# A transformer block on one core: the attention branch's output product as a Strassen product, with operands prepared in the projections and kept in DRAM

## The chip, the cores and the metric

The kernel runs on one core of one Trainium2 chip. The metric is device microseconds (us) from one launch to its end. Before the change three runs gave 1318.06, 1318.31 and 1318.65 us; the median is 1318.31 us.

## What is computed

One residual block of a streaming encoder: 1024 positions, width 1024, float32. Every sub-layer is normalised before and after.

```python
proj = h @ w_in                       # q, k, v, f, g_b, g_c, hc, gate_conv, gate_attn
ya = g_b * conv3(g_c * hc)            # [1024, 512]
yb = forgetting_attention(q, k, v, logf)              # [1024, 512]
ya_d = ya @ w_branch[0]               # branch a, [1024, 512] x [512, 1024]
yb_d = yb @ w_branch[1]               # branch b, [1024, 512] x [512, 1024]
merged = sigmoid(gate_conv) * ya_d + sigmoid(gate_attn) * yb_d
x = x + rmsnorm(merged @ w_out)       # then a SwiGLU feed-forward, same pattern
```

## The kernel before

Activations lie transposed: width on the 128 partitions, positions along the free axis in two halves of 512 (`n1`, `n2`). Each float32 operand is split into a rounded part `hi` and a rest `lo` (`split`, lines 131 to 134: a copy on ScalarE, ACT, and a subtraction on VectorE, DVE). A product is then three matmuls, hi·hi, hi·lo, lo·hi (`mm3`, lines 136 to 142). The large products (projections, w_out, feed-forward) are Strassen products in Winograd's form: a 2 x 2 block product from seven block products, with sums of weight blocks S1 to S4 and of activation blocks T1 to T4. The names A11, B21, T2 and so on are those blocks.

**Projections** (the loop at lines 999 to 1086). Seventeen jobs and a last one of another form. Job 0 to 3 makes a pair of q and k tiles, 4, 5, 7 and 8 the convolution's input (`z`), 6 and 9 its gate (`gb`), and 10 to 17 the two output gates. Each job is a Strassen product of seven times 12 matmuls, 128 x 512 each (`strassen`, lines 639 to 665). TensorE (PE) writes into PSUM banks b1, b2 and b3, and DVE adds these into c12, c22 and c21; bank b2 is rewritten by product S3 after DVE has taken S2's result out. While a job runs, DVE also prepares the next job's weight sums, and `wo_load` (lines 963 to 988) prepares a piece of w_out: four loads of 128 x 128, four sums for T1 to T4, one split, two stores to `wo_dram`. The finished output gates are stored to `sg_dram` (lines 1073 to 1082).

**Attention** (lines 1090 to 1360) works through steps t. Two tables, `cuts` and `at`, say in which step a side work is done: the splits of branch a's operands, the loads of the gates, and in steps 19 to 25 the loads and splits of branch b's four weight tiles (`load_wb`, `split_wb`).

**Branch b** (lines 1448 to 1471). For each half n and each of 8 width tiles d: load the gate `sg` from `sg_dram` (tiles from four buffers, line 1107), 12 matmuls into a fresh PSUM bank `pbb`, then on DVE `sg = sg * pbb` and `um += sg`. In the first half, `cut_wo` loads and splits the plain blocks B11 and B21 of w_out; in the second half the prepared T2 and T1 are loaded. After tile 1 of the second half come `first_ops(0)`, which splits the first blocks of `um`, and `sums(0)`, four sums over `um` on GpSimd (POOL).

**w_out** (lines 1517 on). `first(i)` is the product A11·B11 of position pair i into a bank `p1`, `second(i)` A12·B21 into a bank `q`, four pairs in all. Then come transposes and the other five products. B22 is loaded and split at lines 1622 to 1627.

Each engine executes its own instructions in order. A scheduler chooses that order from dependencies and priorities, except where `strict` (lines 64 to 81) names an engine: its instructions then keep the program's order. Tiles come from pools of fixed size; a tile waits until the last reader of the buffer's previous tile is done. All recorded operations have the line of one helper, so the profile shows nearly everything as L76 (L77 after the change), and groups are told apart by tile names.

Of the kernel before, what the change touches and what calls it, by code (L numbers as in the profile page):

```python
# [10 lines left out]
F32 = mybir.dt.float32  # L11
# [31 lines left out]
B11, B21, B22, T1, T2, T3, T4 = range(7)  # L43


@with_exitstack
def block_kernel(
# [58 lines left out]
    def f32(ap):  # L106
        return ap.bitcast(F32)
# [23 lines left out]
    def split(hi, lo, src):  # L131

        copy(hi, src)
        sub(lo, src, f32(hi))
# [25 lines left out]
    wo_dram = dpool.tile([4, 4, P, 2, NC], F32, name="wo_dram")  # L160
# [802 lines left out]
    def wo_load(n):  # L963
# [12 lines left out]
        def cut():  # L976
            for o, a, b in ((4, 0, 1), (5, 3, 4), (6, 3, 0), (7, 2, 5)):
                sub(r[:, o], r[:, a], r[:, b])
            split(h[:, 4:], l[:, 4:], r[:, 4:])

        def store():
            for hl, t in enumerate((h, l)):
                nc.scalar.dma_start(
                    wo_dram[:, k, :, hl, c * P : (c + 1) * P].rearrange("o p m -> p o m"),
                    f32(t[:, 4:]),
                )
# [3 lines left out]
    side = {}  # L990
# [8 lines left out]
    for ij, (kind, j, _, _) in enumerate(jobs):  # L999
        mid = None  # L1000
        if ij in side:
            cut, store = side.pop(ij)
            mid = do(pinned, cut, "vector", "scalar")
# [79 lines left out]
        if mid is not None:  # L1083
            pinned(store, "scalar")
        if ij < len(jobs) - 2:
            side[ij + 1] = wo_load(ij)
# [8 lines left out]
    yb = yb_pool.tile([P, 4, S], F32, name="yb")  # L1095
# [140 lines left out]
    wbr = {}  # L1236
    wbh, wbl = [], []
# [6 lines left out]

    def load_wb(k):
        wbr[k] = flat(wtile("sx", 1) if k == 3 else raw_t())
        nc.sync.dma_start(wbr[k], w_branch[0, 1][k * P : (k + 1) * P, :])

    def split_wb(k):
        wbh.append(flat(hi_t()))  # L1250
        wbl.append(z_tile("wbl", F32R) if k == 1 else flat(lo_t()))
        return halve(wbh[k], wbl[k], wbr[k])
# [13 lines left out]
    for k, t in enumerate((20, 22, 24, 25)):  # L1266
        cuts[t].append(do(split_wb, k))
# [10 lines left out]
    for k in range(4):  # L1278
        at[19].append(do(load_wb, k))
# [88 lines left out]
    def yb_split(n, ks):  # L1368
        ns = (n1, n2)[n]
        for k in ks:  # L1370
            split(yb2[n][0][:, k, :], yb2[n][1][:, k, :], yb[:, k, ns])

    for m in branch_a(KT - 1, 0, psm, "mm"):
        pass
    for n in range(2):
        nc.scalar.activation(sgs[KT - 1, n], sgs[KT - 1, n], AF.Sigmoid)
    m()
    yb2 = [halves_of(0)]
    for m in branch_a(KT - 2, 1, psm, "mm"):
        pass  # L1380
    yb_split(0, (0, 1))
    m()
    for m in branch_a(KT - 1, 1, psm, "mm"):
        pass
    divide(3, 0)
    yb_split(0, (2, 3))
    m()
    divide(3, 1)
    yb2.append(halves_of(1))
    yb_split(1, range(4))  # L1390
    strict[0] = ()
    yb_close()
    wx, wx_close = pool("wx", side="right")

    def x_tile(n, p=None):
        return (p or wx).tile([P, 2, 4, NC], F32R, tag=f"x{n}", name=f"x{n}", bufs=1)
# [6 lines left out]
    def load_wo(o, k):  # L1403
        nc.sync.dma_start(f32(wo[o][:, :, k, :]), wo_dram[o - T1, k])

    def cut_wo(w, ops):
        for h, (o, row, cols) in enumerate(ops):
            wr = w[:, (n1, n2)[h]]
            nc.sync.dma_start(wr, wout_d[row * P : (row + 1) * P, cols])
            split(*(wo[o][:, hl, row % 4, :] for hl in range(2)), wr)  # L1410

    for n, o in enumerate((B11, B21, T2, T1)):
        wo[o] = x_tile(n)
    loads = [(o, k) for o in (T2, T1) for k in range(4)]
# [19 lines left out]

    def minus(i, o, a, b, op=ALU.subtract):
        e = nc.vector if i else nc.gpsimd
        e.tensor_tensor(o, a, b, op=op)
# [9 lines left out]

    for n in range(2):
        ns = slice(n * NC, (n + 1) * NC)
        for d in range(KT):  # L1450
            ds_ = slice(d * P, (d + 1) * P)
            sg = sg_tile()
            nc.sync.dma_start(sg, sg_dram[d][1, :, ns])
            if n:
                load_wo(*loads.pop(0))
            elif d % 2 == 0:
                cut_wo(flat(raw_t()), ((B11, d // 2, n1), (B21, 4 + d // 2, n1)))
            if d == KT - 1:
                nc.scalar.activation(sg, sg, AF.Sigmoid)
            ps = psm.tile([P, NC], F32, tag="mm", name="pbb")  # L1460
            for k in range(4):
                mm3(
                    ps, (wbh[k][:, ds_], wbl[k][:, ds_]),
                    (yb2[n][0][:, k, :], yb2[n][1][:, k, :]),
                    k == 0, k == 3,
                )
            mul(sg, sg, ps)
            add(um[:, d, ns], um[:, d, ns], sg)
            if n and d == 1:
                first_ops(0, [s4h_t(), s4h_t()], [s4l_t(), s4l_t()])  # L1470
                sums(0, s4_t())
# [153 lines left out]
    for k in (0, 2):  # L1625
        w = ep.tile([P, D], F32, tag="t", name="wr", bufs=1)
        cut_wo(w, ((B22, 4 + k, n2), (B22, 5 + k, n2)))
# [177 lines left out]
    wx_close()  # L1805

# [250 lines left out]
```

## Time and profile before

| what | value |
| --- | --- |
| median of three runs | 1318.31 us |
| span of the profiled execution | 1316.7 us |
| that execution's time outside the span, if it ran at the median | 1.6 us |
| PE busy | 99% |
| DVE busy | 73% |
| ACT busy | 42% |
| POOL busy | 11% |
| mean rate of DMA | 160 GB/s |

The profile is of one execution. Its page gives busy shares by engine and the chain of work that ended last; the trace gives each instruction's start and duration. The listed duration of a matmul is longer than the distance to the next one, since they are pipelined; the distance is what counts. DVE's listed durations overlap in the same way by about 0.1 us.

### The profile page before, as it was taken

Reading aid. Unit: us, or ns where it says so; the run is one execution under the profiler, and the core shown is the slowest. Engines: PE = TensorE matmul, PEld = TensorE weight load, DVE = VectorE, ACT = ScalarE, POOL = GpSimd, SP = SyncE. Lnnn points to the kernel's source line nnn. Section 1 sums busy time; section 2 is a strip of 40 time slices with the busy share of each in tenths; the row PEclk is TensorE's granted clock in tenths of the full one; section 3 lists DMA queues with packets and bytes.
Section 4 is the critical chain, followed back from the end, with each engine's and each line's share of the span. In section 5 each row is a group of like instructions: output and inputs, shape, how many; then the busy total and the mean of one; then the engine's idle time right before and its main releaser. Section 6 shows DMA issues by size and latency. Waiting matters only on the chain.

```text
span 1316.7 us, 17979 instructions
## 1 busy us (share of the span) xinstructions
PE 1307.0 (99%) x6710; PEld 1090.6 (83%) x6710; DVE 964.2 (73%) x1514; ACT 556.4 (42%) x895; POOL 142.0 (11%) x271
## 2 busy tenths in 40 slices
PE   9999999999999999999999999999999999999997
PEld 9988888888888888888888888888888888888886
DVE  6974878765656876776798789987766776676685
ACT  6642322243355866514677522222222234444452
POOL 0001000011012212010012021221001110000000
PEclk9999999999999999999999999999999999999999
DMA  6344544555536545565266555553323337866441
GB/s 215 115 120 136 149 124 121 155 159 150 152 120 200 162 137 175 160 226 208 79 227 206 155 166 176 179 181 104 98 86 120 105 112 285 311 252 193 159 168 64
DMA packets 189351, 211.00 MB, mean 160 GB/s; under 512 B 11584, under 2 KB 137600, under 8 KB 189264
## 3 DMA queue, kind: packets, MB, share of 16 engines
q1 hardware_dynamic: 155872, 146.64, 35.8%
q0 software_dynamic: 16496, 54.83, 11.3%
q10 hardware_dynamic: 16896, 8.39, 2.1%
q8 instruction: 52, 0.85, 0.3%
q14 instruction: 35, 0.29, 0.1%
HBM read 151.30 MB, written 58.52 MB: 159 GB/s over the span
## 4 chain that ended last, share of the span: by engine, by line
PE 95%; DVE 2%; ACT 1%; DMA 1%; issue 0%; DVEq 0%; POOL 0%; ACTq 0%; SPq 0%; POOLq 0%
PE b L76 57%; PE pd L76 16%; PE pbb L76 3%; PE pba L76 3%; PE pv L76 3%; PE po L76 2%; PE tps L76 2%; PE p L76 2%; PE sp L76 2%; PE ma L76 1%; PE tp L76 1%; PE q L76 1%; DMA lo<-qk_dram 1%; PE mb L76 1%; PE spin L76 1%
## 5 line engine op out<-in xcount | busy, mean ns | idle before, releaser
L76 PE MATMUL b<-x,hi 128*128 128x512 f32 x1088 | 335.3, 389 | 0.0
L76 PEld LDWEIGHTS b<-x,hi 128*128 128x128 f32 x1088 | 204.2, 188 | 42.1
L76 PE MATMUL b<-x,lo 128*128 128x512 f32 x544 | 211.7, 389 | 0.0
L76 DVE TENSOR_TENSOR c<-c,b 128x512 f32<-128x512 f32 x193 | 131.8, 683 | 62.1 <-PE b L76 54.6
L76 DVE TENSOR_TENSOR lo<-raw,hi 128x1024 fp32r<-128x1024 f32 x92 | 110.9, 1205 | 76.7 <-PE b L76 66.8
L76 ACT ACTIVATE hi<-raw 128x1024 fp32r<-128x1024 f32 (+1 forms) x99 | 100.5, 1018 | 97.4 <-PE b L76 51.2
L76 PEld LDWEIGHTS b<-x,lo 128*128 128x128 f32 x544 | 102.2, 188 | 21.2
L76 ACT ACTIVATE hi<-sx 128x1024 fp32r<-128x1024 f32 (+1 forms) x43 | 44.9, 1043 | 152.5 <-PE b L76 144.8
L76 ACT ACTIVATE sgf<-c 128x512 f32<-128x512 f32 x31 | 19.6, 633 | 131.8 <-DVE c L76 112.6
L76 DVE TENSOR_TENSOR lo<-sx,hi 128x1024 fp32r<-128x1024 f32 (+1 forms) x43 | 51.5, 1199 | 30.7 <-PE b L76 27.3
L76 DVE TENSOR_TENSOR sx<-raw 128x512 f32<-128x512 f32 x78 | 53.6, 688 | 14.2 <-DMA raw<-in_w_gate_up_dram 6.9
L76 PE MATMUL pd<-hi,lo 128*128 128x512 f32 x160 | 62.3, 389 | 0.0
L76 PE MATMUL pd<-hi 128*128 128x512 f32 x160 | 61.9, 390 | 0.0
L76 PE MATMUL pd<-ghi 128*128 128x512 f32 x148 | 57.6, 390 | 0.0
L76 PE MATMUL pd<-glo,ghi 128*128 128x512 f32 x148 | 57.6, 389 | 0.0
L76 PE MATMUL pd<-ghi,glo 128*128 128x512 f32 x148 | 57.6, 389 | 0.0
L76 PE MATMUL b<-hT34h,lo 128*128 128x512 f32 x136 | 52.9, 389 | 0.0
L76 PE MATMUL b<-hT34h,hi 128*128 128x512 f32 x136 | 52.9, 389 | 0.0
L76 PE MATMUL b<-hT34l,hi 128*128 128x512 f32 x136 | 52.9, 389 | 0.0
L76 PE MATMUL b<-hT12h,hi 128*128 128x512 f32 x136 | 52.9, 389 | 0.0
L76 PE MATMUL b<-hT12l,hi 128*128 128x512 f32 x136 | 52.9, 389 | 0.0
L76 PE MATMUL b<-hT12h,lo 128*128 128x512 f32 x136 | 52.9, 389 | 0.0
(425 smaller groups left out, 3018.3 us busy)
## 6 DMA issues: line engine op xcount, KB each, us to landing
raw<-in_w_gate_up_dram SPq DMA_DIRECT2D x55, 512.0 KB, 3.9
raw<-in_w_in_dram SPq DMA_DIRECT2D x35, 512.0 KB, 4.3
a_dramS<-um POOLq DMA_DIRECT2D x44, 256.0 KB, 3.0
a_dramA<-um POOLq DMA_DIRECT2D x33, 256.0 KB, 2.7
sg<-sg_dram SPq DMA_DIRECT2D x32, 256.0 KB, 3.8
x<-wo_dram SPq DMA_DIRECT2D x16, 512.0 KB, 6.1
graw<-a_dramS SPq DMA_DIRECT2D x14, 512.0 KB, 4.2
sg_dram<-c POOLq DMA_DIRECT2D x24, 256.0 KB, 3.5
```

The lines of the kernel that those rows point to most:

```text
L76: ins = getattr(self.engine, name)(*args, **kw)
```

## The change

Branch b becomes a Strassen product. Its 2 x 2 blocks are: width outputs even and odd tiles, positions `n1` and `n2`, and the 512 inputs in two halves. The seven block products (four width tiles u, two input tiles, three matmuls each, so 24 matmuls) stand in the order A11·B11, S1·T1, S2·T2, S3·T3, S4·B22, A22·T4, A12·B21; TensorE keeps the program's order in them. They accumulate in eight PSUM banks, `pbanks` (tiles `pbp`) and `vbanks` (tiles `pbv`).

Weight blocks: `wb_load` prepares A11, A12, A22 and S1 to S4 in jobs 2 to 9 (four loads of 64 KB, four 128 x 128 sums, a split of 128 x 896, two stores to `wb_dram`); `load_wbr` loads them. `wo_load` splits and stores all seven blocks of w_out, 128 x 896 where it was 128 x 512, and `load_wo` loads B11, B21 and B22 as finished halves, so `cut_wo` is gone. Activation blocks T1 to T4 are formed in place in `yb` on DVE, T1 in attention steps 20 and 22. The T1 block of w_out is loaded into the space of `yb`, its T2 block into that of the temporaries.

```diff
-    wo_dram = dpool.tile([4, 4, P, 2, NC], F32, name="wo_dram")
+    wo_dram = dpool.tile([7, 4, P, 2, NC], F32, name="wo_dram")
+    wb_dram = dpool.tile([7, 2, P, 4, 2, P], F32, name="wb_dram")
...
-            split(h[:, 4:], l[:, 4:], r[:, 4:])
+            split(h[:, 1:], l[:, 1:], r[:, 1:])
...
+    def wb_load(n):
...
+        def cut():
+            add(r[:, 4], r[:, 0], r[:, 3])
+            sub(r[:, 6], r[:, 1], r[:, 0])
+            sub(r[:, 5], r[:, 4], r[:, 1])
+            sub(r[:, 7], r[:, 2], r[:, 5])
+            split(h[:, 1:], l[:, 1:], r[:, 1:])
...
         if ij < len(jobs) - 2:
-            side[ij + 1] = wo_load(ij)
+            side[ij + 1].append(wo_load(ij))
+        if 1 <= ij < 9:
+            side[ij + 1].append(wb_load(ij - 1))
...
+    def load_wbr(o):
+        h = hi_t()
+        l = kblk(z_tile("wbl", F32R)) if o == S1 else lo_t()
+        wb[o] = h, l
+        for hl, t in enumerate((h, l)):
+            nc.sync.dma_start(
+                f32(t).rearrange("p (u k) m -> p u k m", u=4), wb_dram[o, hl]
+            )
...
-    for k, t in enumerate((20, 22, 24, 25)):
-        cuts[t].append(do(split_wb, k))
+    cuts[20].append(cut_b11)
+    cuts[22].append(cut_t1)
...
-    for k in range(4):
-        at[19].append(do(load_wb, k))
+    at[20].append(form_t1)
+    for o, t in ((A11, 19), (S1, 20), (S2, 24), (S3, 25)):
+        at[t].append(do(load_wbr, o))
...
+    def prod_b(ps, o, u, b, first):
+        (wh, wl), (bh, bl) = wb[o], tb[b]
+        kw = {} if first else dict(skip_group_check=True)
+        for k in range(2):
+            m = 2 * u + k
+            mm3(
+                ps, (wh[:, m, :], wl[:, m, :]), (bh[:, k, :], bl[:, k, :]),
+                first and k == 0, k == 1, **kw,
+            )
+
+    def merge(d, ns, t, c, sg):
+        mul(t, c, sg)
+        add(um[:, d, ns], um[:, d, ns], t)
...
+    for u in range(4):
+        prod_b(pbanks[u], S2, u, T2, False)
+        copy(u_s[u], pbanks[u])
+    load_wbr(A12)
+    for u in range(4):
+        sg = gate(2 * u + 1, n1)
+        prod_b(pbanks[u], S3, u, T3, False)
+        add(v_s[u], v_s[u], pbanks[u])
+        merge(2 * u + 1, n1, v_s[u], v_s[u], sg)
+    for u in range(4):
+        sg = gate(2 * u, n1)
+        prod_b(vbanks[u], S4, u, B22, False)
+        add(u_s[u], u_s[u], vbanks[u])
+        copy(vbanks[u], p_s[u])
+        merge(2 * u, n1, u_s[u], u_s[u], sg)
+        load_wo(B21, u)
+    first_ops(0, [s4h_t(), s4h_t()], [s4l_t(), s4l_t()])
+    sums(0, s4_t())
+    for u in range(4):
+        sg = gate(2 * u + 1, n2)
+        prod_b(pbanks[u], A22, u, T4, False)
+        merge(2 * u + 1, n2, sg, pbanks[u], sg)
+    for u in range(4):
+        sg = gate(2 * u, n2)
+        prod_b(vbanks[u], A12, u, B21, False)
+        merge(2 * u, n2, sg, vbanks[u], sg)
...
-        cut_wo(w, ((B22, 4 + k, n2), (B22, 5 + k, n2)))
+    for k in range(4):
+        load_wo(B22, k)
```

Two places where instructions stand in another order. First DVE at the end of branch b, before: `pbb` are PSUM banks, `um` the merged activations, `lo` the split for the second pair of w_out.

```order
L76 TENSOR_TENSOR um_3751<-um_3751,sg_5887 128x512
L76 TENSOR_TENSOR sx_6010<-um_3751 128x512
L76 TENSOR_TENSOR sg_5905<-sg_5905,pbb_5908 128x512
L76 TENSOR_TENSOR um_3751<-um_3751,sg_5905 128x512
L76 TENSOR_TENSOR sg_5923<-sg_5923,pbb_5926 128x512
L76 TENSOR_TENSOR um_3751<-um_3751,sg_5923 128x512
L76 TENSOR_TENSOR sg_5941<-sg_5941,pbb_5944 128x512
L76 TENSOR_TENSOR um_3751<-um_3751,sg_5941 128x512
L76 TENSOR_TENSOR lo_6012<-um_3751,hi_6011 128x1024
L76 TENSOR_TENSOR sg_5959<-sg_5959,pbb_5963 128x512
```

The same place after the change, where the product A22·T4 ends in banks `pbp` and A12·B21 in banks `pbv`:

```order
L77 TENSOR_TENSOR sg_5994<-pbp_5760,sg_5994 128x512
L77 TENSOR_TENSOR sg_6004<-pbp_5761,sg_6004 128x512
L77 TENSOR_TENSOR s4l_5984<-um_3872,s4h_5982 128x512
L77 TENSOR_TENSOR um_3872<-um_3872,sg_5994 128x512
L77 TENSOR_TENSOR um_3872<-um_3872,sg_6004 128x512
L77 TENSOR_TENSOR sg_6014<-pbp_5762,sg_6014 128x512
L77 TENSOR_TENSOR sg_6024<-pbp_5763,sg_6024 128x512
L77 TENSOR_TENSOR um_3872<-um_3872,sg_6014 128x512
L77 TENSOR_TENSOR um_3872<-um_3872,sg_6024 128x512
L77 TENSOR_TENSOR lo_6119<-um_3872,hi_6118 128x1024
L77 TENSOR_TENSOR sg_6035<-pbv_5812,sg_6035 128x512
L77 TENSOR_TENSOR sg_6045<-pbv_5813,sg_6045 128x512
```

The split `lo` for w_out's second pair now stands behind the merges of A22·T4 and ahead of those of A12·B21. The pool gives `p1`, the bank of `first(0)`, the space of `pbv_5813`, whose reader is the last row shown; before the change it gave it the space of `pbb_5926`, whose reader is the fifth row of the first list.

Second, DVE in job 6 of the projections, up to the first add of job 7's second product (`c12` with bank `b2`). Before:

```order
L76 TENSOR_TENSOR sx_2097<-raw_2089,raw_2095 128x512
L76 SCALAR_TENSOR_TENSOR ot_2074<-zt_1916,cw_141,ot_2074 128x512
L76 TENSOR_TENSOR raw_2095<-raw_2095 128x512
L76 TENSOR_TENSOR c22_1997<-ot_2074,c22_1997 128x512
L76 TENSOR_TENSOR sx_2097<-raw_2095,raw_2089 128x512
L76 TENSOR_TENSOR c12_2144<-c21_2128,b2_2130 128x512
L76 TENSOR_TENSOR s4_2109<-raw_2089,sx_2097 128x512
```

After, where `br` and `bl` belong to `wb_load`:

```order
L77 TENSOR_TENSOR br_1989<-br_1989 128x128
L77 TENSOR_TENSOR c12_2051<-ot_2136,c12_2051 128x512
L77 SCALAR_TENSOR_TENSOR ot_2142<-zt_1975,cw_142,ot_2142 128x510
L77 TENSOR_TENSOR bl_1991<-br_1989,bh_1990 128x896
L77 TENSOR_TENSOR c21_2035<-ot_2142,c21_2035 128x512
L77 TENSOR_SCALAR ot_2148<-zt_1975,cw_142 128x512
L77 TENSOR_TENSOR sx_2180<-raw_2172,raw_2178 128x512
L77 SCALAR_TENSOR_TENSOR ot_2148<-zt_1975,cw_142,ot_2148 128x512
L77 TENSOR_TENSOR raw_2178<-raw_2178 128x512
L77 SCALAR_TENSOR_TENSOR ot_2148<-zt_1975,cw_142,ot_2148 128x512
L77 TENSOR_TENSOR sx_2180<-raw_2178,raw_2172 128x512
L77 TENSOR_TENSOR c22_2065<-ot_2148,c22_2065 128x512
```

Behind these twelve rows follow `s4_2192` and then the add `c12_2227<-c21_2211,b2_2213`: the four `br` sums, `bl` and `s4` now stand ahead of that add.

More of the change, by code (lines that the diff above doesn't have):

```diff
@@ L43 @@
 B11, B21, B22, T1, T2, T3, T4 = range(7)
+A11, A12, A22, S1, S2, S3, S4 = range(7)
 @with_exitstack
@@ L1403, in load_wo @@
     def load_wo(o, k):
[L1404 to L1414, printed above, removed]
+        nc.sync.dma_start(f32(wo[o][:, :, k, :]), wo_dram[o, k])
     PAIRS = ST // 2
@@ L1446, in sums @@
         minus(i, a12, a12, a11)
-    for n in range(2):
[L1449 to L1471, printed above, removed]
+    wo[B11], wo[B21] = x_tile(0), x_tile(1)
@@ new lines, in block_kernel @@
+    split(*tb[T3], yb12)
+    tb[B21] = tuple(
+        t0_.tile([P, S], F32R, tag="p", name="b21", bufs=2).rearrange("p (k c) -> p k c", k=2)
+        for _ in range(2)
+    )
+    split(*tb[B21], yb21)
+    sub(yb21, yb21, yb22)
+    split(*tb[T4], yb21)
+    vbanks = [psm.tile([P, NC], F32, tag="mm", name="pbv") for _ in range(4)]
+    for u in range(4):
+        prod_b(vbanks[u], S1, u, T1, True)
+        copy(v_s[u], vbanks[u])
+        load_wo(B11, u)
+    load_wbr(A22)
+    for u in range(4):
+        prod_b(pbanks[u], S2, u, T2, False)
+        copy(u_s[u], pbanks[u])
@@ L1624, in block_kernel @@
     wob[B22] = both(wo[B22])
[L1625 to L1627 removed]
+    for k in range(4):
+        load_wo(B22, k)
     def f_src(f):
```

134 lines of the change are left out of this document (92 added, 42 removed).

## The prediction

> **What bounds the kernel now.** I read the page first, then PE's waits, then the chain of work that ended last. The page:
>
> ```profile
> span 1316.7 us, 17979 instructions
> PE 1307.0 (99%) x6710; PEld 1090.6 (83%) x6710; DVE 964.2 (73%) x1514; ACT 556.4 (42%) x895; POOL 142.0 (11%) x271
> ```
>
> All that PE waited for in the span, the two longest entries of its waits:
>
> ```profile
> PE spin L76 <- POOL ident masks.py:199: 1.5, 1, 1.5
> PE tp L76 <- ACT um L76: 0.6, 1, 0.6
> ```
>
> PE is the bound everywhere, and it has almost no waits. Work that leaves PE therefore shortens the kernel one for one, unless PE now has to wait for somebody. The chain around branch b, start, length and matmuls:
>
> ```profile
> 542.37 10.91 PE pba L76 x48
> 553.28 43.52 PE pbb L76 x192
> 596.80 5.44 PE p L76 x24
> 602.24 2.72 PE q L76 x12
> ```
>
> Branch b is 192 matmuls in 43.52 us, 0.2267 us each, without a gap. Then PE goes straight on with w_out, first(0) and first(1) (24 matmuls, 5.44 us). How close DVE and DMA are to their limits there (busy us of PE, PEld, DVE, ACT, POOL, the clock, the DMA share and GB/s):
>
> ```profile
> 553.00:575.00 22.00, 22.00 (x99) 18.23 (x98) 18.89 (x31) 7.74 (x14) 1.28 (x1) 1.00 0.76 256
> 575.00:597.00 22.00, 22.00 (x99) 18.23 (x98) 16.04 (x21) 2.33 (x3) 5.97 (x5) 1.00 0.43 146
> ```
>
> DVE, at 16 to 19 of 22 us, is the second bound, and the clock is full. The question is whether DVE's side of the Strassen form fits beside PE.
>
> **Part 1: PE's work, minus 5.44 us.** Seven products of 24 matmuls are 168; 24 fewer by 0.2267 are 5.44 us. With nothing in the way the products start at 553.28, 558.72, 564.16, 569.60 (S3), 575.04 (S4), 580.48 (A22) and 585.92 (A12), and PE is ready for w_out at 591.36 where it was at 596.80.
>
> **Part 2: the merges, plus 5.0 us.** What DVE needs per operation, start to start, from its timeline:
>
> ```profile
> 568.59 0.68 DVE L76 TENSOR_TENSOR sg<-sg,pbb 128x512 f32<-128x512 f32 x1
> 569.19 0.68 DVE L76 TENSOR_TENSOR s4l<-um,s4h 128x512 fp32r<-128x512 f32 x1
> 569.79 0.68 DVE L76 TENSOR_TENSOR um<-um,sg 128x512 f32<-128x512 f32 x1
> 570.39 0.68 DVE L76 TENSOR_TENSOR sg<-sg,pbb 128x512 f32<-128x512 f32 x1
> 571.11 0.69 DVE L76 TENSOR_TENSOR um<-um,sg 128x512 f32<-128x512 f32 x1
> ...
> 595.66 1.23 DVE L76 TENSOR_TENSOR lo<-um,hi 128x1024 fp32r<-128x1024 f32 x1
> 596.83 0.69 DVE L76 TENSOR_TENSOR sg<-sg,pbb 128x512 f32<-128x512 f32 x1
> ```
>
> A 128x512 operation takes 0.60, one that needs its predecessor 0.72, a 128x1024 one 1.17. Before, a group of 12 matmuls (2.72 us) brought two merge operations. Now, in S3 and S4, every 6 matmuls (1.36 us) bring three: add the PSUM bank, multiply by the gate, add to um, 1.80 us. DVE falls behind by 0.44 us a group, and A22 and A12 with two per group (1.20 of 1.36) hardly let it catch up, all the more as first_ops' splits stand among them. Following DVE's rows: its first S3 add is at 571.0, the second, held by PE, at 572.4; from there 23 operations (the rest of S3 and S4 and one s4l) run without idle time, 23 x 0.60 = 13.8, to 586.2. Then come the nine rows up to lo (5.4, to 591.6), lo itself (1.17, to 592.8) and the two multiplications that read pbv_5812 and pbv_5813 (1.2), to 594.0. The first matmul of first(0) needs the bank that the second of them reads. Before, its bank had been read out long ahead. So PE waits from 591.36 to 594.0 even in the undisturbed case, 2.6 us.
>
> It will not be undisturbed. POOL's sums(0) follow the last n1 merge, so they now start near 586 and lie beside exactly these nine rows. What they did to DVE before:
>
> ```profile
> 576.70 5.13 POOL L76 TENSOR_TENSOR um<-um 128x512 f32<-128x512 f32 x3 [9.18 <-DVE um L76]
> ```
> ```profile
> 577.26 1.73 DVE L76 TENSOR_TENSOR s4l<-um,s4h 128x512 fp32r<-128x512 f32 x1
> 578.91 0.67 DVE L76 TENSOR_TENSOR sg<-sg,pbb 128x512 f32<-128x512 f32 x1
> 579.61 1.07 DVE L76 TENSOR_TENSOR um<-um,sg 128x512 f32<-128x512 f32 x1
> 580.60 0.68 DVE L76 TENSOR_TENSOR sg<-sg,pbb 128x512 f32<-128x512 f32 x1
> 581.31 1.07 DVE L76 TENSOR_TENSOR um<-um,sg 128x512 f32<-128x512 f32 x1
> ```
>
> Three DVE operations with two operands in SBUF took 1.04, 0.38 and 0.38 us longer, 1.8 together; those that read PSUM did not. There are four such sums, so I take 1.8 + 0.6 = 2.4 us: bank free at 596.4, PE waits 5.0 us. The bounds are 2.6 (no disturbance) and 6.8 (each of the four sums costs the worst row's 1.04).
>
> The Trainium skill, "SBUF — State Buffer", section "SBUF: two separate sides", says that a GpSimd instruction that reads SBUF and a VectorE instruction with two SBUF inputs exclude each other for a whole instruction. The rows agree: only such operations were held, each until about a POOL instruction's end. Stepping through the nine rows by that rule, with 1.28 us for a POOL sum, I estimate the bank free at 596.9, a wait of 5.5 instead of 5.0 us.
>
> **Part 3: the projections, plus 0.8 us.** In jobs 2 to 9 each job gets four more 128x128 sums, a split of 128x896 and a wider w_out split. Rows of DVE in job 6, and PE's first matmul of job 7's S3 product:
>
> ```profile
> 195.31 0.49 DVE L76 TENSOR_SCALAR ot<-zt,cw 128x512 f32<-128x512 f32 x1 [0.83 <-DMA ya_dram<-ot]
> 195.77 0.70 DVE L76 TENSOR_TENSOR r<-r 128x128 f32<-128x128 f32 x3
> ...
> 197.65 0.68 DVE L76 TENSOR_TENSOR l<-r,h 128x512 fp32r<-128x512 f32 x1
> 198.25 0.68 DVE L76 TENSOR_TENSOR c<-ot,c 128x512 f32<-128x512 f32 x1
> 198.85 1.22 DVE L76 TENSOR_TENSOR lo<-raw,hi 128x1024 fp32r<-128x1024 f32 x1
> 199.99 0.68 DVE L76 TENSOR_TENSOR c<-c,b 128x512 f32<-128x512 f32 x1
> ...
> 205.98 0.68 DVE L76 TENSOR_TENSOR c<-c,b 128x512 f32<-128x512 f32 x1
> ```
> ```profile
> 208.51 0.39 PE L76 MATMUL b<-hT34h,hi 128*128 128x512 f32 x1
> ```
> ```profile
> 200.00:219.05 19.05, 19.05 (x86) 15.78 (x85) 17.15 (x29) 5.28 (x7) 1.10 (x2) 1.00 0.46 143
> ```
>
> A small sum costs 0.2. 896 columns lie between 0.60 and 1.14, so about 1.0. Per job that is 0.8 + 1.0, and 0.4 for the wider split, 2.2 us; in a 19.05 us job with DVE at 17.15 (listed durations, which overlap by about 0.1 each) it just fits. But the order matters in the two gb jobs, where DVE had a backlog already: the add of 205.98 frees bank b2 for S3, which starts at 208.51 (0.45 later now, since two matmuls are pulled ahead of it). The add moves by 2.2 and by 0.6 for the s4 that passes it, to end at 209.4 to 209.5. PE waits about 0.5 us, and by a like count some 0.3 in job 9 to 10. Bounds: nothing, if a wait for a transfer, as the 0.83 us at 195.31, absorbs it, and 1.6. The ACT side of these splits and the stores have cover: ACT was busy 5.28 of 19.05.
>
> **Part 4: the rest.** In attention, form_t1 puts 1.2 us of DVE ahead of the row maxima of one step, against two splits less in later steps: 0.2 us (0 to 0.5). The removed cut_wo was hidden behind PE; it frees ACT and DVE at 553 to 565, but DVE's backlog begins at 571, so it gains nothing. The early products get their operands in time. The activation blocks are formed behind the last division of yb:
>
> ```profile
> 551.20 0.69 DVE L76 TENSOR_TENSOR yb<-yb,rb 128x512 f32<-128x512 f32 x1
> ```
>
> From there DVE's order has three operations of 0.60 and seven of 1.17 up to T2's low part, 10.0 us, so 561.2, three us before the product S2·T2 (564.16); what exceeds that, PE would wait. By tile sizes SP's queue moves about 13.5 MB from 545 to 592 (weights, w_out blocks, twelve gates), 290 GB/s; what the DMA engines can keep up is shown between 590 and 640, in slices of 1.25 us:
>
> ```profile
> GB/s 223 0 13 0 0 69 301 383 352 385 406 400 408 405 410 405 424 405 272 8 0 0 0 0 224 207 2 0 0 0 0 0 0 0 0 0 7 0 0 7
> ```
>
> Some 400, so transfers are late only where their buffers come free late. After first(0) DVE's rows stand ahead of need again, so I count no second wait.
>
> **Sum.** −5.44 + 5.0 + 0.8 + 0.2 = +0.6 us. On the profiled execution 1316.7 + 0.6 = 1317.3 of span, and with the 1.6 us outside it 1318.9 us, against the median of 1318.31. A measurement of this kernel can tell about 0.2% (2.6 us) from no change.
>
> **Rivals.** 1. *The merges hide after all* (faster). For it: POOL's sums may start late and miss the nine rows. Against it: DVE's 1.80 us beside PE's 1.36 us in each group of S3 and S4. If only the bank wait falls away, the next wait is for lo_6119 by first(1), about 0.5 us: −5.44 + 0.5 + 1.0 = −3.9, 1314.4 us. If all falls away, 1312.9. From my +0.6, 3.2 us less are needed to count as faster, for instance the wait at 2.6 instead of 5.0 and the projections at nothing. Chance 0.28.
> 2. *The gates come late* (slower). The transfers of sg wait for one of four buffers:
>
> ```profile
> sg<-sg_dram SPq DMA_DIRECT2D x32, 256.0 KB, 3.8
> x<-wo_dram SPq DMA_DIRECT2D x16, 512.0 KB, 6.1
> ```
>
> The gate of pbv_5813 goes into the buffer that A22's second um addition frees, near 591. With 3.8 us it lands at 594.8, in time for its row at 595.8. With the 6.1 of the w_out loads that stand between the gates in SP's queue it comes at 597.1, and the wait grows to 6.5. The kernel becomes slower once it takes over about 7 us, since the gate of A22's last tile, freed near 585.6, then comes late as well; with 8 us it lands at 599, the bank is free at 599.8 and the wait is 8.4: −5.44 + 8.4 + 1.0 = +4.0, 1322.3 us. Chance 0.20.
> My forecast, a wait of about 3 to 7 us at first(0) that eats the gain, has the rest, 0.52.
>
> **How the numbers follow.** The known bounds give −5.44 + 2.6 + 0 = −2.8 to −5.44 + 6.8 + 2.1 = +3.5, 1315.5 to 1321.8. To keep no more than 2 in 10 out I reach into both rivals: 1314.8 to 1322.0. Faster 0.28, same 0.52, slower 0.20.
>
> **What would show it.** In the profile after: pba's end at the same distance from the first product, seven products of 5.44 us, then a gap of about 5 us ahead of the first p with DVE as its releaser, sg<-pbv behind POOL's sums; DVE without idle time from 571 (as counted there) to that gap; short waits of PE for DVE in jobs 7 and 10. It is wrong if p follows A12's last matmul directly, if DVE idles among the merges, if its releaser is a DMA, or if PE waits several us in the projections.

## The result and the profile after

The changed kernel takes 1338.18 us (median of four runs, 1336.71 to 1339.74) against 1318.48 us for the kernel before, measured beside it: a ratio of 1.015, interval 1.0136 to 1.0165. That is 19.7 us slower, where 1318.9 us with a range of 1314.8 to 1322.0 was forecast.

The first lines of the page after:

```profile
span 1337.7 us, 18116 instructions
PE 1308.7 (98%) x6686; PEld 1087.5 (81%) x6686; DVE 983.8 (74%) x1549; ACT 567.8 (42%) x902; POOL 141.8 (11%) x271
```

The span grew by 21.0 us, while PE has 24 instructions less. The chain of work that ended last (start, length, matmuls) tells in which stage:

```profile
404.42 2.72 PE ma L77 x12
...
570.17 5.44 PE pbp L77 x24
...
615.07 7.89 PE p L77 x24
622.96 2.72 PE q L77 x12
```

`ma` is the first matmul of the projections' last job, into which attention's first steps are woven. Before, this row stood at another time:

```profile
388.19 2.72 PE ma L76 x12
```

It begins 404.42 − 388.19 = 16.2 us later: so much is lost in the seventeen jobs ahead of it, called the projections from here on. Branch b begins at 570.17 instead of 553.28, 16.9 us later, and `q` at 622.96 instead of 602.24, 20.7 us later. So branch b with the first matmuls of w_out loses 3.8 us, attention 0.7. PE's waits (us in total, times, longest):

```profile
PE p L77 <- DVE sg L77: 6.8, 1, 6.8
PE b L77 <- DVE lo L77: 6.5, 1, 6.5
PE b L77 <- ACT c L77: 3.0, 3, 1.3
PE b L77 <- DVE c L77: 1.6, 2, 1.4
```

The first row is the wait at first(0) that the prediction had. The other three, 11.1 us, lie in the projections, and there it had 0.8 us. What such a wait costs shows in PE's rows:

```profile
286.15 0.39 PE L77 MATMUL b<-hT12l,hi 128*128 128x512 f32 x1
293.08 0.80 PE L77 MATMUL b<-hT12h,lo 128*128 128x512 f32 x1 [6.54 <-DVE lo L77]
293.67 0.63 PE L77 MATMUL b<-hT12h,hi 128*128 128x512 f32 x1
294.10 0.63 PE L77 MATMUL b<-hT12l,hi 128*128 128x512 f32 x1
```

In a full stream a matmul starts 0.227 us behind the one before it. Here the first distance is 6.93 us, 6.7 more than that. The matmuls behind it start 0.43 us apart, until 298.8, and that adds 2.8 us. A window of ten microseconds (us of PE with its matmuls, PEld, DVE, ACT, POOL; clock, DMA share, GB/s) shows that the granted clock was lowered there; in the next ten it was 0.76:

```profile
284.00:294.00 10.00, 3.46 (x14) 2.59 (x13) 5.00 (x7) 2.03 (x3) 0.54 (x1) 0.73 0.60 166
```

The same window before, with no wait in it:

```profile
284.00:294.00 10.00, 10.00 (x46) 8.29 (x45) 6.73 (x12) 4.50 (x6) 1.08 (x2) 1.00 0.42 125
```

So the wait listed with 6.5 us cost 9.5. Counted in the same way, from start to start, PE lost 1.5 to 1.6 us in each of four other places, 6.2 in all, where the list has 4.6 us (3.0 for ACT and 1.6 for DVE): some 0.4 us more than listed in each. 9.5 and 6.2 are 15.7 of the 16.2 us.

**The wait of 6.5 us, followed back.** First the chain after, ahead of that wait:

```profile
267.78 11.60 DMA wb_dram<-bl
279.89 9.09 DMA raw<-in_w_in_dram
...
291.89 1.15 DVE lo L77
293.08 111.34 PE b L77 x478
```

A store of branch b's new weight blocks leads to a load of `w_in`, that to DVE, and DVE to PE. SP's queue in the projections has this entry among its waits:

```profile
SPq L77 <- DMA wb_dram<-bh: 7.9, 1, 7.9
```

And SP's timeline shows what was behind it:

```profile
269.74 0.33 SPq L77 DMA_DIRECT2D q<-qk_dram  x1
278.15 1.64 SPq L77 DMA_DIRECT2D cb<-c_dram  x2
279.89 0.64 SPq L77 DMA_DIRECT2D raw<-in_w_in_dram  x1
```

`cb` are two rows that attention needs far later. In the code they take the same two buffers in which `wb_load` makes `bh` and `bl`, so SP held their load until these had been stored. The load of the next job's `w_in` stood behind them in the same queue. Before, with these buffers free, SP had issued the load of `cb` much earlier, and nothing waited for it:

```profile
164.98 0.81 SPq L76 DMA_DIRECT2D cb<-c_dram  x2
```

So the change had moved that load behind `wb_load`'s last pieces. DVE's timeline has the price, 11 us without work:

```profile
289.00 0.69 DVE L77 TENSOR_TENSOR sx<-raw 128x512 f32<-128x512 f32 x1 [11.03 <-DMA raw<-in_w_in_dram]
```

`w_in`'s load, once issued, took 9.09 us to land (the chain above), so part of DVE's idle time is the load's own; p_cbpin below tells the two apart.

**The stores took longer to land.** DMA issues in the projections, after (times issued, size, median us from issue to landing):

```profile
raw<-in_w_in_dram SPq DMA_DIRECT2D x32, 512.0 KB, 5.4
wo_dram<-l ACTq DMA_DIRECT2D x16, 448.0 KB, 7.0
wb_dram<-bl ACTq DMA_DIRECT2D x8, 448.0 KB, 9.0
```

Before:

```profile
raw<-in_w_in_dram SPq DMA_DIRECT2D x32, 512.0 KB, 4.3
wo_dram<-l ACTq DMA_DIRECT2D x16, 256.0 KB, 4.2
```

**ACT's queue holds up its own copies.** ACT's timeline in a job with both cuts, and behind it PE's row:

```profile
243.61 0.69 ACTq L77 DMA_DIRECT2D wb_dram<-bh  x1
247.59 0.37 ACTq L77 DMA_DIRECT2D wb_dram<-bl  x1
248.00 0.63 ACT L77 ACTIVATE s4h<-s 128x512 fp32r<-128x512 f32 x1 [4.94 <-DMA wo_dram<-l]
248.54 0.58 ACT L77 ACTIVATE c<-b 128x512 f32<-128x512 f32 x1
```
```profile
249.17 0.50 PE L77 MATMUL b<-hB21h,hi 128*128 128x512 f32 x1 [1.29 <-ACT c L77]
```

The issue of the last store came 3.3 us after the one ahead of it had ended, and `c<-b`, the copy that empties a PSUM bank, stands behind it on ACT. `bl` was ready by then (DVE's row for it is at 243.20, 1.08 us long). The trace's semaphore events show for what ACT waited: this store counts its completion on the same semaphore as a load of `br` that SP had issued at 242.45, and ACT went on when that load had landed, at 247.52. In the four jobs ahead of this one there is no such wait, but the issue of `wb_dram<-bl` itself took 1.39, 1.62, 1.65 and 1.96 us, where it is 0.37 here. ACT, busy for a third of its time in these jobs (37.34 of 114.00 us, in a row at the end), was late all the same.

### The profile page after: what moved, and what is told of

Same layout as the page of the kernel before. It is cut to its first block, busy times and chain, and to the rows that moved or that the text cites. A ratio compares the mean times of both kernels' runs of the same rounds, so it can differ in the third digit from the quotient of the medians.

```text
span 1337.7 us, 18116 instructions
## 1 busy us (share of the span) xinstructions
PE 1308.7 (98%) x6686; PEld 1087.5 (81%) x6686; DVE 983.8 (74%) x1549; ACT 567.8 (42%) x902; POOL 141.8 (11%) x271
## 4 chain that ended last, share of the span: by engine, by line
PE 77%; issue 13%; DMA 4%; DVE 4%; ACT 1%; POOL 1%; SPq 0%; DVEq 0%; POOLq 0%; ACTq 0%
PE b L77 42%; PE pd L77 16%; PE pba L77 3%; PE pv L77 3%; PE p L77 2%; PE po L77 2%; PE tps L77 2%; PE sp L77 2%; PE pbp L77 1%; DMA wb_dram<-bl 1%; PE ma L77 1%; PE q L77 1%; PE tp L77 1%; DMA lo<-qk_dram 1%; DMA raw<-in_w_in_dram 1%
## 5 line engine op out<-in xcount | busy, mean ns | idle before, releaser
L77 DVE TENSOR_TENSOR lo<-raw,hi 128x1024 fp32r<-128x1024 f32 x90 | 108.2, 1202 | 71.5 <-PE b L77 61.2
L77 ACT ACTIVATE hi<-raw 128x1024 fp32r<-128x1024 f32 (+1 forms) x96 | 97.2, 1015 | 85.1 <-PE b L77 46.4
```

What stands on the lines that cost most here:

```text
L77: ins = getattr(self.engine, name)(*args, **kw)
```

## The experiments

Four theories were open. *Queue*: the `cb` load waits for `wb`'s stores and holds up `w_in` behind it. *Traffic*: the larger stores make everything land later. *Vector work*: the cuts put DVE and ACT behind, above all in the two `gb` jobs. And for branch b: the wait at first(0) is DVE's backlog, or the gates.

### The projections alone, and their two halves

**p_all.** The kernel before with all of the new preparation; branch b stays plain.

```diff
+            side[ij + 1].append(wo_load(ij))       # 7 blocks split and stored
+        if 1 <= ij < 9:
+            side[ij + 1].append(wb_load(ij - 1))   # stored, and never read
```

> The kernel before, with all the new preparation in the projections (wb_load's loads, sums, splits and stores, and wo_load's split and stores for seven blocks), and nothing of it used in branch b, which stays as it was. If the loss of the change lies in the projections, last_pair's first matmul starts near 404 us (388.2 before, 404.4 after the change) and the time is near 1318.5 + 16 = 1334 to 1335 us. If the loss of the projections needs the rest of the change, it stays below 1325.

Measured: 1334.49 us, ratio 1.0126 (1.0111 to 1.0141), `ma` at 403.74. The preparation alone costs 15.9 of the 19.7 us, with the same wait of 6.5 us for `lo`, and 3.8 us for ACT's `c`. The Strassen product itself isn't needed for them.

**p_nostore.** As p_all, with the same loads, sums and splits, but only the four old blocks of w_out are stored and nothing to `wb_dram`.

```diff
-                    f32(t[:, 1:]),
+                    f32(t[:, 4:]),
...
-                nc.scalar.dma_start(wb_dram[:, hl, :, u, kk, :]..., f32(t[:, 1:]))
```

> The same preparation without its added stores: all sums and splits are made, the new loads too, but only the four blocks of w_out of before are stored. Traffic theory (the stores of 512-byte pieces fill the DMA engines, w_in's loads land late, and DVE and PE wait): most of the 16 us is gone, 1318 to 1321 us. Vector theory (DVE's sums and splits delay the adds that free PE's banks, the step of the prediction): as much as with the stores, 1330 us and more; by the prediction's own count +0.8 us.

Measured: 1320.73 us, ratio 1.0019 (1.0009 to 1.0028), `ma` at 390.79. Two waits are left, from PE's timeline:

```profile
209.50 0.50 PE L76 MATMUL b<-hT34h,hi 128*128 128x512 f32 x1 [1.03 <-DVE c L76]
...
268.10 0.50 PE L76 MATMUL b<-hT34h,hi 128*128 128x512 f32 x1 [1.16 <-DVE c L76]
```

These are the two places of the prediction's part 3, S3's first matmul behind the two `gb` jobs. The vector work costs 2.2 us there, not 0.8, above the prediction's bound of 1.6, and PE has no other wait in the projections.

**p_storeonly.** The other half: the sizes and number of the new stores, but without the new splits. The stores take the unsplit sums, so T1 to T4 of w_out aren't split.

```diff
-            split(h[:, 1:], l[:, 1:], r[:, 1:])
+            split(h[:, 4:], l[:, 4:], r[:, 4:])
...
-            for hl, t in enumerate((h, l)):
+            for hl, t in enumerate((r, r)):
```

> The stores alone: DVE and ACT do in the projections what they did before (no sums and no split for the branch's weights, the split of w_out's sums at 128x512), but the four stores of 448 KB per job 2 to 9 are issued, from the unsplit tile, so w_out's T blocks are not split rightly. Traffic theory: most of the loss stays, 1328 to 1335 us. Vector theory: about 1319.

Measured: 1324.19 us, ratio 1.0043 (1.0028 to 1.0058), `ma` at 394.47, between what the two theories gave. PE has one wait, 4.3 us for DVE's `lo` at 170.14. The chain ahead of it:

```profile
142.69 12.43 DMA wb_dram<-r
...
159.50 6.86 DMA raw<-in_w_in_dram
...
170.14 9.90 PE b L76 x36
```

`cb` has no shared buffer to wait for in this kernel. But its stores read `r` itself, so the next load into that buffer waits on SP for the store (12.43 us until it landed; SP's longest wait of this kind was 8.2 us), and `w_in`'s load stands behind it. It is the mechanism of the wait at 293 us with another load in front, made by this run's own edit. So its 5.6 us are not a price of traffic alone; they show that long stores are enough for this wait, without any new split. With the 2.2 us of p_nostore they are far from the 15.9 of p_all: the parts don't add up.

**p_wb and p_wo7.** The same preparation cut the other way: `wb_load` alone, and the wider pieces of w_out alone.

```diff
# p_wb
+        if 1 <= ij < 9:
+            side[ij + 1].append(wb_load(ij - 1))
# p_wo7
-            split(h[:, 4:], l[:, 4:], r[:, 4:])
+            split(h[:, 1:], l[:, 1:], r[:, 1:])
```

> The kernel before with wb_load alone (its loads, sums, split and two stores in jobs 2 to 9), w_out's four blocks as before, nothing of it used. Together with p_wo7 it divides the 15.9 us of p_all. If the costs add up, wb_load has about three quarters of it by its bytes in jobs 2 to 9 (14 blocks of 17 or so): +10 to +13 us. If it is the two together that overfill a job, each alone costs a few us, +3 to +6 here.

> The kernel before with only w_out's pieces split and stored for seven blocks, 16 jobs. If the costs add up, +3 to +5 us. If the two together overfill a job, less than +1.5 us.

Measured: p_wb 1323.33 us, ratio 1.0037 (1.0023 to 1.0051), with a wait of 2.3 us for `lo` at 283.12; p_wo7 1318.02 us, ratio 0.9998 (0.9989 to 1.0007). Wider pieces of w_out are free by themselves, the new blocks of branch b cost 5.0 us, and the two together 15.9. That each takes the slack that the other would have used is the likely reason, which no run shows by itself. Most of p_wb's 5.0 us is the held queue again: SP waited there 9.2 us for a store of `bh`, ahead of `cb`, and with the lowered clock behind its wait PE lost 4.2 us between 280 and 287.

**p_pieces.** As p_all, with `wb_dram` and `wo_dram` laid out so that a partition's seven blocks are one stretch of 3.5 KB, where they were seven of 512 bytes.

```diff
-    wb_dram = dpool.tile([7, 2, P, 4, 2, P], F32, name="wb_dram")
+    wb_dram = dpool.tile([2, 4, 2, P, 7, P], F32, name="wb_dram")
...
-                    wb_dram[:, hl, :, u, kk, :].rearrange("o p m -> p o m"), f32(t[:, 1:])
+                    wb_dram[hl, u, kk], f32(t[:, 1:])
```

> All the new preparation, but both DRAM tensors are laid out so that a store writes 3.5 KB per partition in one piece, where it was seven pieces of 512 bytes (the loads of w_out's T blocks then read 512-byte pieces). If the number of pieces makes the traffic slow, most of the 16 us goes: 1318 to 1324 us. If the bytes or the waits of the issuing queue do, it stays at 1330 to 1335.

Measured: 1328.81 us, ratio 1.0076 (1.0061 to 1.0091), 5.7 us less than p_all, `ma` at 396.86. The stores land sooner, `wb_dram<-bl` in 7.1 us (9.2 in p_all) and `wo_dram<-l` in 3.9 (7.3):

```profile
wo_dram<-l ACTq DMA_DIRECT2D x15, 448.0 KB, 3.9
```

Same bytes, 5.7 us less: for a part of the loss, how the stores are cut matters. Where p_all has 3.8 us of waits for ACT's `c`, this kernel has none: the issue of `wb_dram<-bl` took 0.64 to 0.71 us in the four jobs named above, and the load of `br` on whose semaphore the last store waits landed 3.1 us after its issue, not 5.1. SP still waited 6.0 us for a store of `bh`, and PE 4.1 for `lo` behind it.

### The queue

**cb_late.** The changed kernel, with the loads of `cb` written two jobs later, in job 14.

```diff
-            if ij == 12:
+            if ij == 14:
                 k_load(0)
```

> The changed kernel, with the loads for attention's first pair (k, q and two broadcast rows cb) issued in job 14 where it was job 12. In the trace after the change SP's queue waits 7.9 us there for a store of wb_dram, because cb takes the buffers of bh and bl, and the next load of w_in stands behind it. Queue theory: that w_in load is on time, the 6.5 us wait of PE for lo at 293 us goes, and with it some 3 us of lowered clock behind it: about 1338 - 9 = 1329 us. Bandwidth theory (the load is late because the DMA engines are full): 1336 us or more.

Measured: 1338.46 us, ratio 1.0152 (1.0137 to 1.0168). SP still waited 7.0 us for `wb_dram<-bh`: the scheduler issued `cb` where it was before. The run says nothing of the theory.

**p_cbpin.** p_all with `cb` truly behind: pinned on SP in job 14, some 65 us later (issued at 342.40).

```diff
             if ij == 12:
                 k_load(0)
                 q_load(0)
-                cb_of(0, 0)
-                cb_of(0, 1)
+            if ij == 14:
+                pinned(do(cb_of, 0, 0), "sync")
+                pinned(do(cb_of, 0, 1), "sync")
```

> As p_all, with the two broadcast loads cb really issued behind w_in's loads (in SP's order they stand five w_in loads later; in cb_late the scheduler had left them where they were, so that run told nothing). Queue theory: the w_in load near 280 us no longer stands behind a load that waits for wb_dram's store, PE's wait of 6.5 us goes and the lowered clock with it: 1334.5 - 9 = 1325 us. Bandwidth theory: 1332 us or more.

Measured: 1326.42 us, ratio 1.0062 (1.0047 to 1.0077), `ma` at 395.74. PE's longest entry in the projections is now 4.5 us for ACT's `c`, in three places, the longest 2.3. The wait for `lo` is gone and 8.1 us come back: its 6.5 us and the 1.6 that the lowered clock behind it had cost in p_all. SP issued that load of `w_in` at 274.61, in p_all at 280.57: 6.0 us are the queue. The rest of the gain is that the load also landed sooner (the three in this stretch took 4.2 to 7.0 us; the one in p_all 8.87), now without `cb`'s 1 MB ahead of it. Two loads that nobody needed yet were half of the loss in the projections.

**pool_store.** The changed kernel with all these stores on POOL's queue, so that ACT's copies have no store ahead of them.

```diff
-                nc.scalar.dma_start(
+                nc.gpsimd.dma_start(
...
-            pinned(store, "scalar")
+            pinned(store, "gpsimd")
```

> The changed kernel, with the stores to wo_dram and wb_dram issued by POOL's queue instead of ACT's. If the stores hold ACT's copies back (PE's 3.0 us of waits for ACT c), those three waits go: about 1335 us. If the bytes on the DMA engines alone decide, 1337 to 1339 us; dearer if POOL's way of storing costs more.

Measured: 1372.56 us, ratio 1.0413 (1.0395 to 1.043). PE waited 21.2 us for `lo` in four places and 11.4 us for DVE's `c`, while its waits for ACT's `c` were 2.5 us in one place. ACT was relieved a little, and something worse took its place: DVE waited 19.7 us, in two places, for stores of `ot` to `ya_dram`. POOL's queue also carries the stores of the finished tiles (`ya_dram`, `sg_dram`), and these now stood behind the new ones, so DVE waited for their buffers.

**no_gb and p_cbpin_nogb.** `wb_load`'s pieces keep out of the two `gb` jobs (2, 3, 4, 5, 7, 8, 10, 11 instead of 2 to 9): no_gb is the changed kernel with cb_late's edit, p_cbpin_nogb is p_cbpin.

```diff
-        if 1 <= ij < 9:
-            side[ij + 1].append(wb_load(ij - 1))
+        if ij + 1 in WB_JOBS:
+            side[ij + 1].append(wb_load(WB_JOBS.index(ij + 1)))
```

> As cb_late, and wb_load's eight pieces are made in jobs 2, 3, 4, 5, 7, 8, 10 and 11, so not in the two gb jobs (6 and 9), whose DVE work is largest. If DVE's backlog in gb jobs is what holds the banks (the prediction's term of 0.8 us, measured as 1.6 us of waits for DVE c, and part of the waits for ACT c), 2 to 4 us less than cb_late, near 1326 us. If only the traffic counts, the same as cb_late.

> As p_cbpin, and wb_load's pieces are made in jobs 2, 3, 4, 5, 7, 8, 10 and 11, not in the gb jobs 6 and 9. If DVE's and ACT's backlog in the gb jobs makes the rest, 1320 to 1322 us; if the traffic of any job with both pieces does, the same as p_cbpin.

Measured: no_gb 1330.35 us, ratio 1.009 (1.0075 to 1.0105), `ma` at 396.46, and the wait for `lo` down to 0.5 us. SP issued `cb` at 311 there, after 5.3 us of waiting for a store of `bh`, and the `w_in` load behind it cost PE only that 0.5 us: the queue was held again, in a job that could bear it. So its 8.1 us below cb_late are mostly the wait for `lo` (5.1 us there), not the 2 to 4 us of the `gb` jobs that were expected. p_cbpin_nogb 1324.67 us, ratio 1.005 (1.0035 to 1.0065): 1.8 us less than p_cbpin, which is near the 2.2 us that p_nostore gave for the `gb` jobs. It was expected at 1320 to 1322. What is left, 6.5 us by the medians, lies for 5.2 us ahead of `ma` (393.40) in the profile, in six short waits, 2.5 us for ACT's `c` and 0.9 for DVE's, and in what each costs beyond its entry.

### Branch b

**b_less.** The changed kernel without the eight DVE additions of `v_s` and `u_s` in S3 and S4 (those terms of the sum are left out). Only DVE's load falls.

```diff
-        add(v_s[u], v_s[u], pbanks[u])
-        merge(2 * u + 1, n1, v_s[u], v_s[u], sg)
+        merge(2 * u + 1, n1, v_s[u], pbanks[u], sg)
```

> The changed kernel without the eight DVE additions that put v_s and u_s to the results of S3 and S4 (those terms are left out of the sum), so that each of these merges has two operations like the others. DVE theory: 8 x 0.60 = 4.8 us less backlog, so the 6.8 us wait ahead of w_out falls to about 2, no lowered clock behind it (p x24 5.4 to 5.9 us), time about 1338 - 7 = 1331 us. Gate theory: the wait stays above 5 us.

Measured: 1335.22 us, ratio 1.0129 (1.0109 to 1.0149); the wait is 3.4 us, half of 6.8 and between what the two theories gave. Eight additions of 0.60 are 4.8 us, of which 3.4 came out: the gate now holds DVE in their place:

```profile
610.56 0.69 DVE L77 TENSOR_TENSOR sg<-pbv,sg 128x512 f32<-128x512 f32 x1 [1.95 <-DMA sg<-sg_dram]
```

**b_nogate.** The changed kernel without the transfers of A22's and A12's gates (the second half's gates are left out; other data is multiplied in).

```diff
-        sg = gate(2 * u, n2)
         prod_b(vbanks[u], A12, u, B21, False)
-        merge(2 * u, n2, sg, vbanks[u], sg)
+        merge(2 * u, n2, u_s[u], vbanks[u], u_s[u])
```

> The changed kernel without the gate transfers of A22 and A12: their merges multiply by what stands in the temporaries, the same number of DVE operations (the second half's attention gates are left out of the result). DVE theory: only the 1.1 us that DVE itself waited for a gate goes, the wait ahead of w_out stays at 5 to 6 us. Gate theory: it falls below 3 us.

Measured: 1334.73 us, ratio 1.0125 (1.0105 to 1.0146); the wait is 4.5 us. Without any gate to wait for, two thirds of it stay. The scheduler also moved `lo` behind the multiplications there, so the difference of 2.3 us is not the gate's price alone: `lo` stood ahead of them for 1.1 us (611.43 to 612.56 after the change), and the gate's 1.08 are the rest.

**a12_second.** The order of the products changed, A12·B21 in second place, so that its merges are long done, and A22 last and from tile 3 down.

```diff
-    load_wbr(S4)
+    load_wbr(S3)
...
-        prod_b(vbanks[u], A12, u, B21, False)
-        merge(2 * u, n2, sg, vbanks[u], sg)
...
+    for u in (3, 2, 1, 0):
+        prod_b(pbanks[u], A22, u, T4, False)
```

> The changed kernel, with the product A12*B21 as the second of the seven (on the banks of A11*B11, its merges beside S1*T1 and S2*T2, where DVE has 7.9 us of idle time), and A22*T4 last, its tiles in reversed order. DVE theory (its 40 merge operations at the end are late): the wait ahead of w_out falls from 6.8 to 1 us or less, p x24 takes 5.4 instead of 7.7 to 7.9 us since the clock isn't lowered, and the time is about 1338 - 8 = 1330 us. Gate theory (the wait is for gate transfers): the gates of the last product are as late, and it stays above 1335 us.

Measured: 1337.22 us, ratio 1.0145 (1.013 to 1.016). The bank is no longer waited for. Another operand of DVE is, from PE's timeline:

```profile
615.13 0.80 PE L77 MATMUL p<-x,lo 128*128 128x512 f32 x1 [6.45 <-DVE lo L77]
```

That was the prediction's "next wait", `lo` of the second pair, priced there at 0.5 us: behind the same backlog it is 6.5.

**b_early.** a12_second, with that split written ahead of A22's merges.

```diff
     first_ops(0, [s4h_t(), s4h_t()], [s4l_t(), s4l_t()])
+    first_ops(1, hi_t(), lo_t())
     sums(0, s4_t())
```

> As a12_second (A12*B21 as the second product), and the split for w_out's second pair stands ahead of A22's merges; it needs only columns that S3 and S4 have finished. In a12_second PE waited 6.45 us for this split in place of the bank. If DVE's order at the end is what holds PE, that wait falls below 1.5 us and branch b, with w_out's start, gains: the time from last_pair's first matmul to the end is about 924 to 926 us (928.5 before, 933.3 after the change, 932.8 in a12_second). If DVE's total work holds it, the wait moves to the next split and the stretch stays above 930.

Measured: 1331.98 us, ratio 1.0113 (1.0096 to 1.013). From `ma` to the end it takes 1329.5 − 401.70 = 927.8 us, where the changed kernel takes 1337.7 − 404.42 = 933.3 and the one before 1316.7 − 388.19 = 928.5. PE still waits there, 2.9 us for `lo` in two places. 924 to 926 was expected. In eight other profiles with the plain branch this stretch takes 928.0 to 929.0 us, so from attention on the Strassen form comes out level with the plain one; a gain of 0.7 us is not shown, and 5.4 is out of reach.

**best.** b_early with `cb` pinned and the pieces kept out of the `gb` jobs.

```diff
+    first_ops(1, hi_t(), lo_t())
...
+                pinned(do(cb_of, 0, 0), "sync")
...
+    WB_JOBS = (2, 3, 4, 5, 7, 8, 10, 11)
```

> b_early's branch b with p_cbpin_nogb's projections: the two parts add up. If the projections cost 3 us and branch b gains 4, about 1317 us, faster than both kernels; if either repair fails, 1320 to 1330 us.

Measured: 1324.02 us, ratio 1.0046 (1.0031 to 1.0061), `ma` at 394.49. That is 14 us faster than the changed kernel and still 6 us slower than the one before: no version found beats the kernel before. From `ma` to the end its profile takes 1324.9 − 394.49 = 930.4 us with the same branch b that took 927.8 in b_early: the two parts did not quite add up.

## Why the prediction was wrong

**Part 1 was right.** The chain after has 24 matmuls in each 5.44 us, and `pba` ends where the first product starts, as before.

**Part 2 had the place and the mechanism; the size was off.** The prediction put DVE's first S3 addition 17.7 us behind the first product (571.0 and 553.28). DVE's rows after, and POOL's:

```profile
587.89 0.69 DVE L77 TENSOR_TENSOR temps<-temps,pbp 128x512 f32<-128x512 f32 x1 [7.85 <-PE pbp L77]
...
600.73 1.18 DVE L77 TENSOR_TENSOR um<-um,temps 128x512 f32<-128x512 f32 x1
...
604.84 0.88 DVE L77 TENSOR_TENSOR s4l<-um,s4h 128x512 fp32r<-128x512 f32 x1
605.64 3.46 DVE L77 TENSOR_TENSOR um<-um,sg 128x512 f32<-128x512 f32 x2
...
610.23 1.27 DVE L77 TENSOR_TENSOR um<-um,sg 128x512 f32<-128x512 f32 x2
...
614.32 0.69 DVE L77 TENSOR_TENSOR sg<-pbv,sg 128x512 f32<-128x512 f32 x1 [1.08 <-DMA sg<-sg_dram]
```
```profile
599.76 1.61 POOL L77 TENSOR_TENSOR s<-um 128x512 f32<-128x512 f32 x1 [17.73 <-DMA sg<-sg_dram]
603.86 4.69 POOL L77 TENSOR_TENSOR um<-um 128x512 f32<-128x512 f32 x3 [2.50 <-DVE um L77]
```

587.89 − 570.17 is 17.72, as worked out, and from there DVE has no idle time until the last multiplication, which PE waits for. POOL's sums held `um<-um,sg`: that pair took 3.46 us, and the next one, after POOL, 1.27, so 2.2 us; with 0.2 on the row of 604.84, the nine rows were held for 2.4 us, just what was taken for them (1.8 measured and a fourth sum assumed, so partly luck). Another 0.5 came on the row of 600.73, ahead of the nine, beside the first of the sums. New is 1.08 us for the gate of the last tile: rival 2's transfer. It took 5.10 us from its issue at 609.13, where the rival needed more than about 7 to make the kernel slower, and so DVE waited one microsecond. So the slower side, which had a chance of 0.20, came by another cause than the one it was given for. The wait was 6.8 instead of 5.0, at the upper end of the bounds of 2.6 to 6.8. The estimate by the Trainium skill, "SBUF — State Buffer", section "SBUF: two separate sides", was 5.5; the held rows agree with that rule again (only operations with two inputs in SBUF took longer, each while POOL ran), and the gate's 1.08 us are most of what the estimate lacked.

**What followed the wait was not in the sum.** The first `p` group, 24 matmuls, took 7.89 us, not 5.44. The windows of the wait and behind it have the clock in the third column from the right:

```profile
608.25:615.00 6.75, 0.00 (x0) 0.00 (x0) 5.67 (x9) 0.00 (x0) 0.81 (x2) 0.84 0.82 270
615.00:623.00 8.00, 7.93 (x25) 6.36 (x26) 8.00 (x14) 4.05 (x6) 0.00 (x0) 0.71 1.01 360
```

So a wait of 6.8 us cost 9.3. Branch b: −5.44 + 6.8 + 2.45 = +3.8 us, what the chain shows. After b_less's wait of 3.4 us the same group took 7.34, after b_nogate's of 4.5 us 7.30.

**Part 3 is the step that failed**: "The ACT side of these splits and the stores have cover: ACT was busy 5.28 of 19.05." With it the stores stood at nothing in the sum and the whole part at 0.8 us, and the projections lost 16.2; that PE would wait several us there was the prediction's own sign of being wrong. Busy time was the wrong measure for two queues that work strictly in order. On ACT, four store issues a job are long or wait for their turn, and the copies that free PSUM banks wait behind them (3.0 us in three places, read from the trace). On SP, the load of `cb` reuses the buffers of `bh` and `bl`; it had moved in the queue and waits for something new (p_cbpin: 8.1 us). The prediction costed neither that move nor the store. Its part 4 had the sentence that fits: transfers are late only where their buffers come free late. It asked that question for branch b and not for the projections. The part that was priced, DVE in the `gb` jobs, came in the two places named and cost 2.2 us (p_nostore), more than the upper bound of 1.6.

What holds ACT's store issues is known in part. One waited for a load's landing, through a shared semaphore (247.59); others were long in themselves, and so they were in p_storeonly, where two issues took 6.9 us without any new split. Both eased when the pieces of the stores were larger, and PE's waits for ACT's `c` went (p_pieces). Without the larger pieces these waits came only where both the new splits and all of the new stores were there (p_all, the changed kernel and those made from them). Why an issue takes 1.4 to 2.0 us instead of 0.4 stays open: moving the stores to another queue (pool_store) brought larger waits and separated nothing.

**Part 4** had attention at +0.2; it is +0.7. The forecast of the sum was +0.6, and it came to 16.2 + 0.7 + 3.8 = 20.7 of the span's 21.0. Rival 1 (all hidden) would have needed DVE's backlog to vanish; even b_early kept 2.9 us of waits for DVE.

## What to carry to other kernels

A side work of DMAs is not covered because its engine is idle: follow each new store to the buffer that it keeps, to the next load that takes this buffer, and to whatever stands behind that load in an in-order queue (in p_all this was half of the loss), and read the new order of the DMA queues as well as that of the busy engines. Price a long wait of TensorE with the slow stretch behind it (6.8 us cost 9.3 here), and a short one with some 0.4 us more than listed. Run the parts of a change alone and together: 0 and 5.0 us made 15.9.

## What the runs showed of the hardware

Behind every wait of 3.4 us and more in a full stream the granted clock fell, in all runs (ahead of w_out, 24 matmuls that take 5.44 us then took 7.3 to 7.9). Behind waits of 2.1 to 2.5 us it fell in five of six cases. One of these and the exception, from cb_late (2.1 us) and p_cbpin (2.3 us):

```profile
208.00:216.00 8.00, 6.25 (x20) 5.00 (x21) 5.88 (x9) 2.29 (x3) 0.56 (x1) 0.79 0.94 287
```
```profile
208.00:216.00 8.00, 5.68 (x26) 4.68 (x26) 6.54 (x10) 2.39 (x4) 0.56 (x1) 1.00 1.02 303
```

The Trainium skill, "TensorE: Matmul & The Clock Gate", section "What's actually happening", has the array go to half its clock after about 3.4 us of idling and back after about as long a busy stretch. The longer waits agree; the five between 2.1 and 2.5 us do not, since the clock fell there after less idling than that. An estimate by that page: the 2.45 us lost after the wait of 6.8 are 4.9 us at half clock, more than one such stretch.

Stores in pieces of 512 bytes took more of the DMA engines' time for the same bytes than stores in pieces of 3.5 KB. One window of the projections, before, after, and in p_pieces (its last two columns are the DMA share and GB/s):

```profile
121.00:235.00 114.00, 114.00 (x507) 94.38 (x506) 85.43 (x139) 31.33 (x40) 5.46 (x10) 1.00 0.46 132
```
```profile
121.00:235.00 114.00, 112.05 (x492) 91.42 (x492) 93.27 (x159) 37.34 (x45) 5.47 (x10) 1.00 0.74 201
```
```profile
121.00:235.00 114.00, 113.42 (x500) 92.86 (x499) 95.26 (x164) 37.68 (x46) 5.48 (x10) 1.00 0.65 205
```

The change raised the share by 61% (0.46 to 0.74) for 52% more bytes (132 to 201 GB/s). p_all has 0.75 at 201 GB/s there, p_pieces 0.65 at 205. Its stores of w_out's low parts landed in 3.9 us (7.3 in p_all), and the kernel was 5.7 us faster than p_all.
